# A hybrid decoder layer on one core: block products of an inverse taken tile by tile in turn, and norms of q by transposes

## The chip, the cores and the metric

The kernel runs on one core of a Trainium2 chip as one launch. The number that counts is the device time of that launch in microseconds (us). Five engines work side by side, each through its own instruction stream in order: TensorE (PE; its weight loads are shown apart as PEld), VectorE (DVE), ScalarE (ACT), GpSimd (POOL) and SyncE (SP), which only issues DMAs here. They wait for one another by semaphores.

## The reference

One decoder layer on 512 positions of width 1024, in float32. A wide input projection feeds two token mixers: a gated DeltaNet (8 heads of 128) and a gated linear recurrence (RG-LRU, 1280 channels). A gated merge, an output projection, a layer norm, a SwiGLU feed-forward part (width 2816) and a second layer norm follow. The part that matters here is the DeltaNet, cut to its core:

```
q = l2_normalize(q); k = l2_normalize(k)        # per position and head, over 128 channels
A = where(strict, (k*beta) @ k.T * decay, 0)    # per chunk and head
T_mat = A + I
sol = triangular_solve(T_mat, [v*beta, k*beta*exp(G)], lower=True, unit_diagonal=True)
o = (q*exp(G)) @ S + (q @ k.T * decay) @ v_new  # and S carried from chunk to chunk
```

## The kernel before

The large products stream 512 positions at a time: a weight block of 128x128 is loaded and a 128x512 operand runs through it. Each float32 product of that kind is taken as three matmuls (`mm3`, lines 154 to 157) on operands that ACT and POOL or DVE split into a high and a low part. A column job of 128 output columns is 8 such triples. The columns of the input projection come in the order of a table (`ORDER`), through `columns` and `play`.

The DeltaNet runs beside them, two heads at a time (four pairs, `dn_chain(p)`), with chunks of 128 positions instead of the reference's 64, so eight 128x128 matrices per pair (4 chunks, 2 heads). PE's program is written out by hand: `play` emits one triple, adds 0.68 to a planned clock and calls `advance`, which emits the next piece of each chain whose planned time has come. A chain gives, after each piece, the planned PE time of the piece and the latency until its result is to be there; the table `LAT` holds these latencies. So a larger number in `LAT` puts the next piece of that chain further down in PE's program, behind more triples; nothing waits by it. Each DVE and ACT instruction is placed by a scheduler, and one inside `with urgent()` gets a higher priority.

The inverse of T_mat is built from small blocks. A substitution on DVE inverts the 16x16 blocks on the diagonal (line 603 on, planned latency `sub`). Then PE doubles the block size: `m1` (line 632) and `m2` (line 644) go from 16 to 32 with products of 32x32 blocks, on four positions (0,0), (32,32), (64,64), (96,96) of the array; `i1`, `i2`, `i3` (lines 671, 683, 693) go from 32 to 64; `i4` and `i5` (lines 701, 710) go from 64 to 128 with 64x64 blocks. Each product stands 8 times, for the eight matrices, and float32 runs it as two passes. Before, a position is finished with all eight products, then triples of the projection follow, then comes the next position.

The norms of k (`norms`, line 490) transpose k on PE, square the transposed bank on ACT and sum it on DVE. The norms of q (`norms_q`, line 502) square q on ACT in the layout it has, and sum over the partitions with a product with ones on PE (tile `qn`, line 508). The result, after a reciprocal root on DVE, scales the output at the end of the chain.

PSUM banks outside the projections come from a ring of five (`bankd`): each use takes the next one, so a bank's new writer waits until the old content was read. `hold` takes a bank out of the ring and `give` puts it back at the end.

Of the kernel before, what the change touches and what calls it, by code (L numbers as in the profile page):

```python
# [8 lines left out]
F32 = mybir.dt.float32  # L9
F32R = mybir.dt.float32r  # L10
I32 = mybir.dt.int32
AF = mybir.ActivationFunctionType
ALU = mybir.AluOpType
# [7 lines left out]
         "z1 l3 v3 q3 g0 z2 g1 l4 g2 g3 z3 g4 g5 g6 g7")  # L21

LAT = {
    "F": 13.0, "kt": 12.0, "q": 5.2, "sq": 4.0, "qk": 1.0, "P": 4.0, "vt": 2.0, "u": 10.0, "sub": 29.0, "m1": 6.0,
    "m2": 8.0, "i2": 6.0, "i4": 7.0, "i5": 7.0, "x": 8.0, "ks": 5.0, "xr": 7.0, "su": 6.5, "ot": 26.0,
    "ba": 9.0, "g": 2.5, "conv": 11.0,
}

PIECE = 0.01
# [3 lines left out]
RMS_EPS = 1e-6  # L33
P = 128
# [7 lines left out]
CQ, CK, CV, CZ, CB, CA = 0, 1024, 2048, 3072, 4096, 4104  # L42
# [4 lines left out]
def layer_kernel(  # L47
# [9 lines left out]
    V, S, G, PE = nc.vector, nc.scalar, nc.gpsimd, nc.tensor  # L57

    const = ctx.enter_context(tc.tile_pool(name="const", bufs=1))
# [25 lines left out]
    def bank(ring, name):  # L85
        tag = rings[ring].pop(0)
        rings[ring].append(tag)
        return pp.tile([P, T], F32, tag=tag, name=name)
# [4 lines left out]
    def bankd(name):  # L93
        return bank("d", name)
# [46 lines left out]
    def rsqrt_seed(y, v):  # L141
        V.tensor_scalar(out=y.bitcast(I32), in0=v.bitcast(I32), scalar1=1, scalar2=None,
                        op0=ALU.logical_shift_right)
        V.tensor_scalar(out=y.bitcast(I32), in0=y.bitcast(I32), scalar1=-1.0,
                        scalar2=float(0x5F3759DF), op0=ALU.mult, op1=ALU.add)

    def rsqrt(y, v, w):
        rsqrt_seed(y, v)
        for _ in range(3):
            tt(V, w, y, y, ALU.mult)  # L150
            stt(w, w, -0.5, v, ALU.mult, ALU.mult)
            stt(y, w, 1.5, y, ALU.add, ALU.mult)
# [237 lines left out]
        V.tensor_scalar(out=c8n, in0=c8, scalar1=-1.0, scalar2=None, op0=ALU.mult)  # L390
        V.memset(tiny, 2.0 ** -110)

    ones = const.tile([P, 4], F32, name="ones")
    V.memset(ones, 1.0)
    eye32 = const.tile([P, 32], F32, name="eye32")
    for b in range(4):
        G.tensor_copy(out=eye32[32 * b:32 * b + 32],
# [45 lines left out]
    qkv = {}  # L443
# [33 lines left out]
    def dn_chain(p):  # L477
# [4 lines left out]
        sml = lambda n, name: small(n, f"{name}{p}", name)  # L482
# [7 lines left out]
        def norms(src, sq, n2, y, name):  # L490

            for j in range(2):
                ps = to_tok(src, j, f"{name}{p}_{j}")
                act(sq[:, j], ps, AF.Square)
                V.tensor_reduce(out=n2[:, 4 * j:4 * j + 4], in_=c4(sq[:, j]), axis=AX.X, op=ALU.add)
                yield j, ps
            V.tensor_scalar(out=n2, in0=n2, scalar1=RMS_EPS, scalar2=None, op0=ALU.add)
            rsqrt(y, n2, sml(8, f"{name}w"))

        c4 = lambda ps: ps.rearrange("p (c n) -> p c n", c=4)  # L500

        def norms_q(qT, sq, n2, y):

            act(sq, qT, AF.Square)
            yield 0.0, LAT["sq"]
            ps = bankd(f"qn{p}")
            for i in range(8):
                PE.matmul(ps[:, 4 * i:4 * i + 4], chunks(sq)[:, i], ones, start=True, stop=True)
            V.tensor_scalar(out=n2, in0=ps[:, 0:32:4], scalar1=RMS_EPS, scalar2=None, op0=ALU.add)
            rsqrt(y, n2, sml(8, "qtw"))  # L510


        yield from until("decay", *([f"k{p - 1}"] if p else []))
        yield from room(2)
        F, Fl = slot(f"F{p}"), slot(f"Fl{p}")
# [21 lines left out]
        nk, rk, nq, rq = (sml(8, n) for n in ("nk", "rk", "nq", "rq"))  # L537
# [12 lines left out]
        for j in range(2):  # L550
            ps = bankd(f"kk{p}_{j}")
            for c in range(4):
                i = 4 * j + c
                PE.matmul(ps[:, c * P:(c + 1) * P], kc[:, i], kc[:, i], start=True, stop=True)
            for c in range(4):
                i = 4 * j + c
                stt(Ac[:, i], ps[:, c * P:(c + 1) * P], br2[:, i:i + 1], Ac[:, i], ALU.mult, ALU.mult)

        def query_chain():
            yield from until(f"{CQ}_{p}")  # L560
            yield from room(1)
            sq, qc = slot(f"sq{p}"), chunks(qkv[CQ, p])
            yield from norms_q(qkv[CQ, p], sq, nq, rq)
            free(sq)
            yield 0.9, LAT["qk"]
            for j in range(2):
                ps = bankd(f"qk{p}_{j}")
                for c in range(4):
                    i = 4 * j + c
                    PE.matmul(ps[:, c * P:(c + 1) * P], kc[:, i], qc[:, i], start=True, stop=True)  # L570
                tt(V, Pm[:, j], ps, Pm[:, j], ALU.mult)
            done[f"q{p}"] = clock[0] + 1.8 + LAT["P"]
            yield 1.8, 0.0
# [26 lines left out]
        X, N = blk(xa, 0), blk(xa, 1)  # L600
        Xh, Ah, R, W = (half(xa, i) for i in (4, 5, 6, 7))
        for b in range(4):
            sl = slice(32 * b, 32 * b + 32)
# [19 lines left out]
        b8 = lambda ps, n: ps[:, :8 * n].rearrange("p (c n) -> p c n", c=8)  # L623
        yield from room(1)
        Yf = slot(f"Yf{p}")
        Yc = chunks(Yf)
        G.memset(Yf, 0.0)
        tag, ps = hold(f"m1{p}")
        for b in range(4):
            sl = slice(32 * b, 32 * b + 32)  # L630
            for i in range(8):
                PE.matmul(b8(ps, 32)[sl, i], N[sl, i], Y[sl, i], start=True, stop=True,
                          tile_position=(32 * b, 32 * b))
            if b < 3:
                yield 0.27, PIECE
        with urgent():
            V.tensor_copy(out=Z, in_=b8(ps, 32))
        give(tag)
        yield 0.27, LAT["m1"]
        tag, ps = hold(f"m2{p}")  # L640
        for b in range(4):
            sl = slice(32 * b, 32 * b + 32)
            for i in range(8):
                PE.matmul(b8(ps, 16)[sl, i], Z[sl, i], X[sl, i, 0:16], start=True, stop=True,
                          tile_position=(32 * b, 32 * b))
            if b < 3:
                yield 0.27, PIECE
        with urgent():
            tt(V, X[:, :, 0:16], X[:, :, 0:16], b8(ps, 16), ALU.subtract)
            V.transpose(out=rows_of(Y), in_=rows_of(X))  # L650
        give(tag)
        yield 0.27, LAT["m2"]
        done[f"s{p}"] = clock[0]
        yield from until(f"v{p}")
        vb = vbs[0]
# [2 lines left out]
        for b in range(4):  # L658
            sl = slice(32 * b, 32 * b + 32)
            G.tensor_copy(out=Yc[sl, :, sl], in_=Y[sl])  # L660
        X6c = flat(xa)[0:64, 256:768].rearrange("p (c n) -> p c n", c=8)
        G.memset(X6c[0:32, :, 32:64], 0.0)
        for b in range(2):
            sl = slice(32 * b, 32 * b + 32)
            G.tensor_copy(out=X6c[sl, :, sl], in_=X[sl])
        Qs = Y
        lohi = [(b, slice(b, b + 32), slice(b + 32, b + 64)) for b in (0, 64)]
        tag, ps = hold(f"i1{p}")
        for b, lo, hi in lohi:
            for i in range(8):  # L670
                PE.matmul(b8(ps, 32)[lo, i], Ac[hi, i, lo], Y[hi, i], start=True, stop=True,
                          tile_position=(b + 32, b))
            if b == 0:
                yield 0.27, PIECE
        with urgent():
            for b, lo, hi in lohi:
                V.tensor_copy(out=Qs[lo], in_=b8(ps, 32)[lo])
        give(tag)
        yield 0.27, LAT["i2"]
        tag, ps = hold(f"i2{p}")  # L680
        for b, lo, hi in lohi:
            for i in range(8):
                PE.matmul(b8(ps, 32)[lo, i], X[lo, i], Qs[lo, i], start=True, stop=True,
                          tile_position=(b, b))
            yield 0.27, PIECE
        with urgent():
            for b, lo, hi in lohi[::-1]:
                V.tensor_scalar(out=Yc[lo, :, hi], in0=b8(ps, 32)[lo], scalar1=-1.0, scalar2=None,
                                op0=ALU.mult)
        give(tag)  # L690
        ps = bankd(f"i3{p}")
        for i in range(8):
            PE.matmul(b8(ps, 32)[32:64, i], Qs[0:32, i], X[0:32, i], start=True, stop=True,
                      tile_position=(0, 32))
        with urgent():
            V.tensor_scalar(out=X6c[32:64, :, 0:32], in0=b8(ps, 32)[32:64], scalar1=-1.0, scalar2=None,
                            op0=ALU.mult)
        yield 0.27, LAT["i4"]
        ps = bankd(f"i4{p}")
        for i in range(8):  # L700
            PE.matmul(b8(ps, 64)[0:64, i], Ac[64:128, i, 0:64], Yc[64:128, i, 64:128], start=True, stop=True,
                      tile_position=(64, 0))
# [5 lines left out]
        ps = bankd(f"i5{p}")  # L708
        for i in range(8):
            PE.matmul(b8(ps, 64)[0:64, i], X6c[:, i], q6[i // 4][:, i % 4], start=True, stop=True,  # L710
                      tile_position=(0, 0))
        with urgent():
            V.tensor_scalar(out=Yc[0:64, :, 64:128], in0=b8(ps, 64)[0:64], scalar1=-1.0, scalar2=None,
                            op0=ALU.mult)
        vt, St = xa, A
# [5 lines left out]
        for c in range(4):  # L721
            ij = [c, 4 + c]
            if c > 0:
                ps = bankd(f"ks{p}_{c}").rearrange("p (j n) -> p j n", j=4)
# [6 lines left out]
            ps = bankd(f"xr{p}_{c}").rearrange("p (j n) -> p j n", j=4)  # L731
# [5 lines left out]
            if c < 3:  # L737
                ps = bankd(f"su{p}_{c}").rearrange("p (j n) -> p j n", j=4)
# [11 lines left out]
        qT = qkv[CQ, p]  # L750
        Pc, qc = chunks(Pm), chunks(qT)
# [29 lines left out]
        for j in range(2):  # L781
            ps = to_tok(obc, j, f"ot{p}_{j}")
# [289 lines left out]
    for i in range(4):  # L1072
        ps = bankp(f"mx1_{i}")
# [112 lines left out]
```

## Time and profile before

| | before |
|---|---|
| device time, median of 3 runs | 1060.07 us (1057.27 to 1061.66) |
| the profiled execution: device time | 1059.51 us |
| its span, first to last instruction | 1057.8 us |
| PE busy | 1032.3 us, 98% |
| DVE, ACT, POOL busy | 537.6, 426.3, 243.2 us |

A row of a view names the engine, the line of the kernel, the operation, the output and input tiles (buffer numbers left out), the shape and a count (x16). A matmul row counts passes: a float32 product of small blocks is two of them. Consecutive instructions of one kind are merged into one row; a row's duration reaches from the first start to the last end, and the ends of matmuls overlap with their successors, so the pace is read from start to start.

### The profile page before, as it was taken

To read this page: it belongs to the slowest core of one execution; us is meant where nothing else is said; L and a number is where in the kernel's file an instruction comes from. 1 tells how busy PE (TensorE), PEld (TensorE's weight loads), DVE (VectorE), ACT (ScalarE), POOL (GpSimd) and SP (SyncE) were. 2 spreads that over 40 slices of the span, in tenths; PEclk is the share of its full clock that TensorE was granted. 3 is DMA by queue.
4 is the path that set the end of the run, shared out by engine and by line. 5 is a ranking of instruction groups with operands and counts; after the bars stand their busy time and mean duration, and the time that the engine had idled before them with its cause. 6 is when DMAs were issued, how large, how long until landed. Compare 5 with 4: busy or idle time off the path is not lost. (4 is left out here: it accounts for less than half of the span.)

```text
span 1057.8 us, 14227 instructions
## 1 busy us (share of the span) xinstructions
PE 1032.3 (98%) x5662; PEld 848.0 (80%) x5662; DVE 537.6 (51%) x1154; ACT 426.3 (40%) x571; POOL 243.2 (23%) x234
## 2 busy tenths in 40 slices
PE   7999999999999999999999999899999999999996
PEld 4887777887887788878888888798888888888885
DVE  3769889645858482247133354933333333322426
ACT  4589256328523743485322224222222222221122
POOL 2373434423433333445400003000000000000006
PEclk9999899999999999999999999999999999999998
DMA  8332222212222222325333436203333433223322
GB/s 245 111 90 68 62 61 71 81 41 71 80 60 64 67 63 77 84 59 147 100 109 91 160 97 181 81 1 88 93 98 100 132 107 99 91 91 99 100 60 79
DMA packets 150662, 96.79 MB, mean 91 GB/s; under 512 B 4475, under 2 KB 139836, under 8 KB 150596
## 3 DMA queue, kind: packets, MB, share of 16 engines
q1 hardware_dynamic: 148064, 91.52, 30.0%
q0 software_dynamic: 1216, 4.20, 1.2%
q8 instruction: 44, 0.72, 0.3%
q10 hardware_dynamic: 1316, 0.16, 0.1%
q14 instruction: 22, 0.18, 0.1%
HBM read 93.76 MB, written 2.11 MB: 91 GB/s over the span
## 5 line engine op out<-in xcount | busy, mean ns | idle before, releaser
L135 ACT CAST wh<-wr 128x1024 fp32r<-128x1024 f32 x145 | 152.3, 1052 | 438.9 <-issue 150.4
L121 POOL TENSOR_TENSOR wl<-wr,wh 128x512 fp32r<-128x512 f32 x128 | 172.9, 1373 | 226.6 <-ACT wh L135 225.1
L121 DVE TENSOR_TENSOR wl<-wr,wh 128x1024 fp32r<-128x1024 f32 x81 | 99.2, 1225 | 209.5 <-ACT wh L135 209.5
L155 PE MATMUL pj<-xT,wh 128*128 128x512 f32 x224 | 93.6, 418 | 0.0
L157 PE MATMUL pj<-xT,wl 128*128 128x512 f32 x224 | 87.6, 391 | 0.0
L156 PE MATMUL pj<-xT,wh 128*128 128x512 f32 x224 | 87.5, 390 | 0.0
L127 ACT ACT_TABLE_LOAD x61 | 78.3, 1283 | 10.6 <-DMA rw<-in_lru_conv_w 7.5
L156 PE MATMUL dn<-wl,fT 128*128 128x512 f32 (+1 forms) x168 | 63.3, 377 | 0.0
L155 PE MATMUL dn<-wh,fT 128*128 128x512 f32 (+1 forms) x168 | 63.3, 377 | 0.0
L157 PE MATMUL dn<-wh,fT 128*128 128x512 f32 (+1 forms) x168 | 63.2, 376 | 0.0
L155 PE MATMUL fg<-hk,wh 128*128 128x512 f32 x160 | 62.3, 389 | 0.0
L156 PE MATMUL fg<-hk,wh 128*128 128x512 f32 x160 | 62.3, 389 | 0.0
L157 PE MATMUL fg<-hk,wl 128*128 128x512 f32 x160 | 62.2, 389 | 0.0
L155 PE MATMUL fu<-hk,wh 128*128 128x512 f32 x160 | 62.2, 389 | 0.0
L156 PE MATMUL fu<-hk,wh 128*128 128x512 f32 x160 | 62.2, 389 | 0.0
L157 PE MATMUL fu<-hk,wl 128*128 128x512 f32 x160 | 62.2, 389 | 0.0
L121 POOL TENSOR_TENSOR h<-h,g 128x512 f32<-128x512 f32 x6 | 8.1, 1357 | 193.2 <-ACT h L127 193.2
L155 PE MATMUL g<-xT,wh 128*128 128x512 f32 x128 | 51.4, 401 | 0.0
L157 PE MATMUL g<-xT,wl 128*128 128x512 f32 x128 | 50.0, 391 | 0.5 <-POOL wl L121 0.5
L156 PE MATMUL g<-xT,wh 128*128 128x512 f32 x128 | 49.9, 390 | 0.0
L157 PEld LDWEIGHTS pj<-xT,wl 128*128 128x128 f32 x224 | 42.1, 188 | 9.2
L155 PEld LDWEIGHTS pj<-xT,wh 128*128 128x128 f32 x224 | 42.1, 188 | 7.9 <-issue 0.2
(358 smaller groups left out, 2283.8 us busy)
## 6 DMA issues: line engine op xcount, KB each, us to landing
wr<-in_w_in SPq DMA_DIRECT2D x64, 512.0 KB, 3.9
wr<-in_w_ffn_gate SPq DMA_DIRECT2D x22, 512.0 KB, 3.8
wr<-in_w_ffn_up SPq DMA_DIRECT2D x22, 512.0 KB, 3.8
wr<-in_w_ffn_down SPq DMA_DIRECT2D x22, 512.0 KB, 3.7
wr<-in_w_branch_lru SPq DMA_DIRECT2D x8, 512.0 KB, 3.9
wr<-in_w_branch_dn SPq DMA_DIRECT2D x8, 512.0 KB, 4.6
wr<-in_w_out SPq DMA_DIRECT2D x8, 512.0 KB, 4.5
wk<-in_w_in SPq DMA_DIRECT2D x8, 256.0 KB, 6.3
```

What stands on the lines that cost most here:

```text
L121: return eng.tensor_tensor(out=o, in0=a, in1=b, op=op)
L127: return S.activation(out=o, in_=i, func=func, **kw)
L135: S.copy(out=hi, in_=src)
L155: PE.matmul(ps, wh, rh, start=start, stop=False)
L156: PE.matmul(ps, wh, rl, start=False, stop=False)
L157: PE.matmul(ps, wl, rh, start=False, stop=stop)
```

## The change

```diff
 LAT = {
-    "F": 13.0, "kt": 12.0, "q": 5.2, "sq": 4.0, "qk": 1.0, ... "sub": 29.0, "m1": 6.0,
+    "F": 13.0, "kt": 12.0, "q": 5.2, "qk": 5.0, ... "sub": 33.0, "m1": 7.0,
...
-    "ba": 9.0, "g": 2.5, "conv": 11.0,
+    "ba": 9.0, "g": 2.5, "conv": 14.0,
...
-    ones = const.tile([P, 4], F32, name="ones")
-    V.memset(ones, 1.0)
...
-        def norms_q(qT, sq, n2, y):
-
-            act(sq, qT, AF.Square)
-            yield 0.0, LAT["sq"]
-            ps = bankd(f"qn{p}")
-            for i in range(8):
-                PE.matmul(ps[:, 4 * i:4 * i + 4], chunks(sq)[:, i], ones, start=True, stop=True)
-            V.tensor_scalar(out=n2, in0=ps[:, 0:32:4], scalar1=RMS_EPS, scalar2=None, op0=ALU.add)
-            rsqrt(y, n2, sml(8, "qtw"))
...
-            yield from norms_q(qkv[CQ, p], sq, nq, rq)
+            for _ in norms(qc, sq, nq, rq, "qt"):
+                pass
...
+        quarters = [slice(32 * b, 32 * b + 32) for b in range(4)]
         tag, ps = hold(f"m1{p}")
-        for b in range(4):
-            sl = slice(32 * b, 32 * b + 32)
-            for i in range(8):
+        for i in range(8):
+            for b, sl in enumerate(quarters):
                 PE.matmul(b8(ps, 32)[sl, i], N[sl, i], Y[sl, i], start=True, stop=True,
                           tile_position=(32 * b, 32 * b))
-            if b < 3:
-                yield 0.27, PIECE
+            if i == 3:
+                yield 0.5, PIECE
...
-        yield 0.27, LAT["m1"]
+        yield 0.5, LAT["m1"]
...
-        tag, ps = hold(f"i1{p}")
-        for b, lo, hi in lohi:
-            for i in range(8):
+        ps = bankd(f"i1{p}")
+        for i in range(8):
+            for b, lo, hi in lohi:
                 PE.matmul(b8(ps, 32)[lo, i], Ac[hi, i, lo], Y[hi, i], start=True, stop=True,
                           tile_position=(b + 32, b))
-            if b == 0:
-                yield 0.27, PIECE
...
-        tag, ps = hold(f"i2{p}")
-        for b, lo, hi in lohi:
-            for i in range(8):
+        ps, p3 = bankd(f"i2{p}"), bankd(f"i3{p}")
+        for i in range(8):
+            for b, lo, hi in lohi:
                 PE.matmul(b8(ps, 32)[lo, i], X[lo, i], Qs[lo, i], start=True, stop=True,
                           tile_position=(b, b))
-            yield 0.27, PIECE
+            PE.matmul(b8(p3, 32)[32:64, i], Qs[0:32, i], X[0:32, i], start=True, stop=True,
+                      tile_position=(0, 32))
...
-        ps = bankd(f"i3{p}")
-        for i in range(8):
-            PE.matmul(b8(ps, 32)[32:64, i], Qs[0:32, i], X[0:32, i], start=True, stop=True,
-                      tile_position=(0, 32))
```

`m2` is changed as `m1` is. So the products of one matrix now stand on the two to four positions one after the other, then those of the next matrix; a piece of `m1` or `m2` holds 16 products (four matrices on four positions) instead of 8, `i1` is one piece of 16, and `i2` and `i3` are one piece of 24. Per pair, 13 pieces become 6. The norms of q go through `norms`, as those of k do.

The first place is PE's program in pair 0, from the norms of q to the norms of k of pair 1. `lw` are the gates of the recurrence, `lg` and `pj` columns of the projection, `qk` the products of k and q, `kt` the transposes of k of pair 1. Before:

```order
L825 MATMUL lw_1_0_812<-u_441,gr_444 128x512
...
L825 MATMUL lw_1_1_818<-u_441,gr_444 128x512
L508 MATMUL qn_856<-ones,sq_801 128x4 x8
...
L570 MATMUL qk_0_898<-x_0_430,x_0_404 128x128 x4
L570 MATMUL qk_1_904<-x_0_430,x_0_404 128x128 x4
...
L487 MATMUL kt_0_919<-ident,x_1_415 128x128 x4
L487 MATMUL kt_1_927<-ident,x_1_415 128x128 x4
```

And of the change:

```order
L807 MATMUL lw_0_0_796<-u_439,gr_442 128x512
L485 MATMUL qt_0_800<-ident,x_0_428 128x128 x4
L485 MATMUL qt_1_807<-ident,x_0_428 128x128 x4
...
L807 MATMUL lw_1_0_836<-u_439,gr_442 128x512
...
L807 MATMUL lw_1_1_842<-u_439,gr_442 128x512
...
L559 MATMUL qk_0_888<-x_0_428,x_0_402 128x128 x4
L559 MATMUL qk_1_894<-x_0_428,x_0_402 128x128 x4
...
L485 MATMUL kt_0_921<-ident,x_1_413 128x128 x4
L485 MATMUL kt_1_929<-ident,x_1_413 128x128 x4
```

Eight products with ones became eight transposes in two banks, and they stand earlier, behind the first of the four `lw`. Counted back five banks, the second bank of `kt` followed on `lw_1_1` before and follows on `lw_1_0` now.

The second place is PE's program in pair 0 from the end of `m1` (tile m_1082 or m_1115) to `m2` (m_1180 or m_1205). Before:

```order
L632 MATMUL m_1082<-xa_564 32x32 x8
L155 MATMUL pj_2_1_1137<-xT_132,wh_979 128x512
...
L487 MATMUL vt_0_1148<-ident,x_0_653 128x128 x4
L487 MATMUL vt_1_1154<-ident,x_0_653 128x128 x4
...
L157 MATMUL pj_2_1_1137<-xT_209,wl_980 128x512
L644 MATMUL m_1180<-xa_564 32x16 x8
L155 MATMUL lx_0_1196<-xT_132,wh_1022 128x512
```

And of the change:

```order
L622 MATMUL m_1115<-xa_562 32x32 x16
L155 MATMUL pj_2_1_1103<-xT_172,wh_981 128x512
...
L485 MATMUL vt_0_1170<-ident,x_0_651 128x128 x4
L485 MATMUL vt_1_1176<-ident,x_0_651 128x128 x4
...
L157 MATMUL lx_0_1189<-xT_172,wl_1025 128x512
L633 MATMUL m_1205<-xa_562 32x16 x16
L155 MATMUL lx_0_1189<-xT_183,wh_1024 128x512
```

`m2` began with the last triple of `pj_2_1` behind it and now begins five triples of `lx` later; `m1` ends later too. A row holds sixteen products where it held eight.

The third place is DVE's program where `m2` of pair 0 gets its bank: the products of k with k of pair 1 (`kk`, tile Fl) have to be read first. `x` are the convolution's taps on `pj_2_0`. Before:

```order
L637 COPY xa_564<-m_1082 128x256
...
L124 SCALAR_TENSOR_TENSOR Fl_757<-kk_0_1040,br_949,Fl_757 128x128
L124 SCALAR_TENSOR_TENSOR x_2_886<-pj_2_0_1027,cols,x_2_886 128x511
L124 SCALAR_TENSOR_TENSOR Fl_757<-kk_0_1040,br_949,Fl_757 128x128
L124 SCALAR_TENSOR_TENSOR x_2_886<-pj_2_0_1027,cols,x_2_886 128x510
...
L124 SCALAR_TENSOR_TENSOR Fl_757<-kk_1_1049,br_949,Fl_757 128x128 x4
```

And of the change:

```order
L124 SCALAR_TENSOR_TENSOR x_2_900<-pj_2_0_1029,cols,x_2_900 128x511
...
L124 SCALAR_TENSOR_TENSOR x_2_900<-pj_2_0_1029,cols,x_2_900 128x509
L627 COPY xa_562<-m_1115 128x256
...
L124 SCALAR_TENSOR_TENSOR Fl_755<-kk_0_1042,br_951,Fl_755 128x128 x4
L124 SCALAR_TENSOR_TENSOR Fl_755<-kk_1_1051,br_951,Fl_755 128x128 x4
```

The three taps moved ahead of the copy of `m1`. Ahead of the four `Fl<-kk_0` DVE has the same instructions as before and two TENSOR_REDUCE of 128x512 more (the sums of the norms of q); a small memset is gone.

## Rows read from the trace of the kernel before

**Rows 1.** The page: span, busy time of each engine, PE's granted clock in 40 slices.
```profile
span 1057.8 us, 14227 instructions
PE 1032.3 (98%) x5662; PEld 848.0 (80%) x5662; DVE 537.6 (51%) x1154; ACT 426.3 (40%) x571; POOL 243.2 (23%) x234
...
PEclk9999899999999999999999999999999999999998
```
**Rows 2.** PE's waits: line, releaser: us in total, times, longest.
```profile
PE kt L487 <- ACT ig L127: 2.0, 1, 2.0
...
PE ks L726 <- DVE Fl L124: 1.3, 2, 0.9
```
**Rows 3.** PE's groups by form: passes, busy us, mean ns of one.
```profile
L632 PE MATMUL m<-xa 32*32 32x32 f32 x256 | 11.0, 192 | 0.0
...
L671 PE MATMUL i<-xa,Fl 32*32 32x32 f32 x128 | 5.5, 192 | 0.0
...
L693 PE MATMUL i<-xa 32*32 32x32 f32 x64 | 2.7, 192 | 0.0
```
**Rows 4.** Timeline, m1 of pair 0 (start, us); last, line 632's loads (min/median/max ns).
```profile
105.29 0.69 PE L632 MATMUL m<-xa 32*32 32x32 f32 x16
105.91 0.50 PE L155 MATMUL pj<-xT,wh 128*128 128x512 f32 x1
106.24 0.39 PE L156 MATMUL pj<-xT,wh 128*128 128x512 f32 x1
106.47 0.40 PE L157 MATMUL pj<-xT,wl 128*128 128x512 f32 x1
106.80 0.69 PE L632 MATMUL m<-xa 32*32 32x32 f32 x16
...
105.29 0.58 PEld L632 LDWEIGHTS m<-xa 32*32 32x32 f32 x16 [0.37 <-issue]
...
L632 PEld LDWEIGHTS m<-xa x256: 101/108/108, 105.3 to 347.8; 32*32 32x32 f32 x128
```
**Rows 5.** Timeline of PE: norms of q, transposes of v, a group of i4.
```profile
81.66 1.84 PE L508 MATMUL qn<-ones,sq 128*128 128x4 f32 x16
83.36 0.48 PE L155 MATMUL lg<-xT,wh 128*128 128x512 f32 x1
...
112.63 1.03 PE L487 MATMUL vt<-ident,x 128*128 128x128 f32 x8
113.42 0.48 PE L155 MATMUL pj<-xT,wh 128*128 128x512 f32 x1
...
157.42 1.14 PE L701 MATMUL i<-Yf,Fl 64*64 64x64 f32 x16
```
**Rows 6.** Timeline of ACT and PE around the wait of kt.
```profile
85.30 0.69 ACT L127 ACTIVATE ig<-lw,cols 128x512 f32<-128x512 f32 x1
...
89.94 0.66 PE L487 MATMUL kt<-ident,x 128*128 128x128 f32 x4 [2.03 <-ACT ig L127]
```
**Rows 7.** Timeline of PE and DVE at m2 of pair 0; one reduce on DVE.
```profile
116.69 0.39 PE L157 MATMUL pj<-xT,wl 128*128 128x512 f32 x1
118.49 0.67 PE L644 MATMUL m<-xa 32*32 32x16 f32 x16 [1.41 <-DVE Fl L124]
...
118.09 1.37 DVE L124 SCALAR_TENSOR_TENSOR Fl<-kk,br,Fl 128x128 f32<-128x128 f32 x5
...
98.52 0.68 DVE L495 TENSOR_REDUCE nk<-xa 128x4 f32<-128x512 f32 x1
```
**Rows 8.** Stretches: us, busy of PE, PEld, DVE, ACT, POOL, PEclk, DMA.
```profile
77.50:119.40 41.90, 38.46 (x258) 30.68 (x257) 40.30 (x124) 27.55 (x33) 15.35 (x13) 1.00 0.26 69
...
117.00:120.00 3.00, 1.59 (x21) 1.08 (x20) 3.00 (x10) 1.73 (x3) 0.43 (x2) 1.00 0.34 101
120.00:130.20 10.20, 10.20 (x65) 7.72 (x65) 7.93 (x26) 1.46 (x3) 6.58 (x13) 0.50 0.19 53
...
165.00:187.00 22.00, 22.00 (x210) 16.67 (x209) 21.36 (x44) 12.70 (x15) 12.63 (x10) 1.00 0.27 73
```
**Rows 9.** Timeline of PE: two groups of m2 of pair 0.
```profile
119.98 1.03 PE L644 MATMUL m<-xa 32*32 32x16 f32 x16
...
122.52 1.03 PE L644 MATMUL m<-xa 32*32 32x16 f32 x16
```

More of the change, by code (lines that the diff above doesn't have):

```diff
@@ L23 @@
 LAT = {
-    "F": 13.0, "kt": 12.0, "q": 5.2, "sq": 4.0, "qk": 1.0, "P": 4.0, "vt": 2.0, "u": 10.0, "sub": 29.0, "m1": 6.0,
+    "F": 13.0, "kt": 12.0, "q": 5.2, "qk": 5.0, "P": 4.0, "vt": 2.0, "u": 10.0, "sub": 33.0, "m1": 7.0,
     "m2": 8.0, "i2": 6.0, "i4": 7.0, "i5": 7.0, "x": 8.0, "ks": 5.0, "xr": 7.0, "su": 6.5, "ot": 26.0,
-    "ba": 9.0, "g": 2.5, "conv": 11.0,
+    "ba": 9.0, "g": 2.5, "conv": 14.0,
 }
@@ L638, in dn_chain @@
         give(tag)
-        yield 0.27, LAT["m1"]
+        yield 0.5, LAT["m1"]
         tag, ps = hold(f"m2{p}")
-        for b in range(4):
-            sl = slice(32 * b, 32 * b + 32)
-            for i in range(8):
+        for i in range(8):
+            for b, sl in enumerate(quarters):
                 PE.matmul(b8(ps, 16)[sl, i], Z[sl, i], X[sl, i, 0:16], start=True, stop=True,
                           tile_position=(32 * b, 32 * b))
-            if b < 3:
-                yield 0.27, PIECE
+            if i == 3:
+                yield 0.5, PIECE
         with urgent():
@@ L651, in dn_chain @@
         give(tag)
-        yield 0.27, LAT["m2"]
+        yield 0.5, LAT["m2"]
         done[f"s{p}"] = clock[0]
@@ L677, in dn_chain @@
                 V.tensor_copy(out=Qs[lo], in_=b8(ps, 32)[lo])
-        give(tag)
-        yield 0.27, LAT["i2"]
-        tag, ps = hold(f"i2{p}")
-        for b, lo, hi in lohi:
-            for i in range(8):
+        yield 0.4, LAT["i2"]
+        ps, p3 = bankd(f"i2{p}"), bankd(f"i3{p}")
+        for i in range(8):
+            for b, lo, hi in lohi:
                 PE.matmul(b8(ps, 32)[lo, i], X[lo, i], Qs[lo, i], start=True, stop=True,
                           tile_position=(b, b))
-            yield 0.27, PIECE
+            PE.matmul(b8(p3, 32)[32:64, i], Qs[0:32, i], X[0:32, i], start=True, stop=True,
+                      tile_position=(0, 32))
         with urgent():
@@ L689, in dn_chain @@
                                 op0=ALU.mult)
-        give(tag)
-        ps = bankd(f"i3{p}")
-        for i in range(8):
-            PE.matmul(b8(ps, 32)[32:64, i], Qs[0:32, i], X[0:32, i], start=True, stop=True,
-                      tile_position=(0, 32))
         with urgent():
-            V.tensor_scalar(out=X6c[32:64, :, 0:32], in0=b8(ps, 32)[32:64], scalar1=-1.0, scalar2=None,
+            V.tensor_scalar(out=X6c[32:64, :, 0:32], in0=b8(p3, 32)[32:64], scalar1=-1.0, scalar2=None,
                             op0=ALU.mult)
-        yield 0.27, LAT["i4"]
+        yield 0.6, LAT["i4"]
         ps = bankd(f"i4{p}")
```

## The prediction

> **What bounds the kernel now.** I read the page first, then PE's waits, then PE's groups by form, then the timeline where small products stand, and last the stretches with their clock. On the page the reader is to see that PE is busy for 98% of the span and no other engine for more than 51% [rows 1]. PE's waits are few and short: 2.0 us at `kt`, 1.3 at `ks`, 1.4 at the first `m2` [rows 2, 7]. So what leaves PE's program leaves the time, unless a wait takes its place. PE's clock is at full speed except in the fifth slice and at the end [rows 1]; the stretches show where: at 120.0 it falls to 0.50, the lower of its two levels (1.2 of 2.4 GHz), for 10.2 us, after 3 us in which PE was busy for 1.59 [rows 8].
>
> The sum is made against the profiled execution: 1059.51 us with a span of 1057.8. The median of the three runs is 1060.07, so 0.56 is added at the end.
>
> **Fewer pieces of small products.** One piece of `m1` (8 products, 16 passes) and one triple repeat every 106.80 - 105.29 = 1.51 us. A matmul of the triple takes 106.47 - 106.24 = 0.23, the triple 0.68. So the piece costs 0.83. Its 16 loads take 0.58 in all; less 0.108 for the last one that is 0.47 for 15 steps, 0.0315 a pass, and 16 passes are 0.50. The other 0.33 is paid once per piece for going into small positions and back: 0.33 instead of 0.23 from the last `pj` to the first `m1`, the same behind the piece, and the rest at its edges [rows 4]. That is one price for all five kinds of piece, whose means are alike [rows 3]. The groups count 256 passes of `m1`, 128 of `i1`, 64 of `i3` [rows 3]; `m2` (16 columns, the same pace [rows 7]) has by the code as many as `m1`, and `i2` as many as `i1`: 832 passes, 52 pieces. The new code has 6 a pair, 24 in all. 28 x 0.33 = 9.2 us go.
>
> **Taking the positions by turns.** The passes stay 832. No row shows a change of position inside a piece, so this is bounded. Today a pass follows the columns of its weights and not those of its operand: 16 moving columns take as long as 32 [rows 4, 7], and 4 take (83.36 - 81.66)/16 = 0.106 us with 128 weight columns; 64 columns take (1.14 - 0.22)/15 = 0.061, with 0.22 for the last pass [rows 5]. Low end: the positions work side by side, four for the 512 passes of `m1` and `m2`, two for the 128 of `i1`, three for the 192 of `i2` and `i3`: 512 x 0.0315 x 3/4 + 128 x 0.0315 / 2 + 192 x 0.0315 x 2/3 = 18.1 us less. High end: each of the 416 changes of position (one per product) costs half of the 0.33 of a whole piece, 416 x 0.165 = 68.6 more. I take a value near the plain pace, because loads that stay serial gain next to nothing: by the paces above 32 columns are 0.0265 (from 128) to 0.0305 (from 64), so 0.001 to 0.005 of the 0.0315 is handing over; 0.0035 hidden at 416 changes is 1.5 us less.
>
> What a group shows here is a price at each entry into small positions. The Trainium skill, "TensorEngine Tiling (Array Packing)", section Key Properties, says that changing the tiling mode drains the array while changing only the tile does not, and that tiles load and multiply in parallel; by it the term would be near the low end, a result that stands among the rivals. The same page, section Restrictions and Gotchas, speaks against: row tiles are not to access one PSUM bank at the same time, and here four row tiles write one bank; by that the term would be nought. No run here shows either yet.
>
> **Norms of q.** The product with ones goes: 1.70 us for 16 passes [rows 5]. Eight transposes come, priced by those of v: 113.42 - 112.63 = 0.79 [rows 5]. 0.91 x 4 pairs = 3.6 us less on PE. ACT squares two banks of 512 instead of 1024 in one go, the same elements, off the path. DVE gets two reduces of 0.68 a pair [rows 7]; what they cost comes next.
>
> **Waits.** `kt` of pair 1 waited for its second bank until the last `ig` was read by ACT, 2.03 us; the order counted back five banks gives it now the bank of the first `ig`, read at 85.99 before [rows 6]. With two Squares in front, 0.7 each as that `ig`, it is 87.4. PE was there at 89.94 - 2.03 = 87.9 and comes 0.9 earlier by the norms, 87.0: 0.4 is left, 1.6 goes.
>
> `m2` of pair 0 waits for its bank until DVE has read the first half of `kk`. In the stretch up to there DVE is busy 40.30 of 41.90 us [rows 8], so it, not PE, sets that moment. Two reduces in front move it by up to 1.36, less the spare of 1.60, of which some lies behind waits that stay. PE comes later too: five triples more in front (3.4), two pieces fewer (0.6), norms (0.9), `kt` (1.6): 0.3 later. So the wait of about 1.5 (a matmul behind the start at 116.69 to 118.49, less the entry) [rows 7] becomes between 1.2 and 2.6; I take 2.1, 0.6 more. Behind the waiting `m2` on PE stand the triples of `lx`; nothing but the recurrence's later chain waits for those. The two together give 1.0 less.
>
> **The clock.** The drop stays: the same wait, no shorter, still stands ahead of the same `m2`. Its price: a piece of `m2` and a triple take 122.52 - 119.98 = 2.54 us in it [rows 9] and 1.51 outside [rows 4], so 10.2 x (1 - 1.51/2.54) = 4.1 us. It is in both sums.
>
> **Latencies.** `sub`, `m1`, `conv` and `qk` only move pieces down in PE's program. They cost nothing while triples remain to stand between: the last `ot` still stands ahead of columns of the merge gates and of `yl` in the new order, as before. SP's broadcast of the decays and POOL's masks move by a place or two, with more than 10 us until their use. If that cover were gone, the price is a wait like that at `ks`, 1.3 [rows 2].
>
> **The sum.** 9.2 + 1.5 + 3.6 + 1.0 = 15.3 us. 1059.5 - 15.3 = 1044.2, with 0.56 for the median 1045.
>
> **Rivals.** *Side by side.* The positions overlap fully: 18.1 instead of 1.5, 1028. For it: four positions use different partitions and their own weights. Against: a product's two passes share a position, and the loads at 0.0315 may come through one port. Anything between 1028 and 1040 counts here.
>
> *The clock falls in more places.* On the other side. A piece of `m1` or `m2` is now twice as long, two of them with a single triple between, at seven places beside the first `m2`. Where the clock falls at one, it costs 4.1. Four of them, 16.4, are more than the 15.3 gained: 1061, no longer faster, and from six on, 24.6, it is slower by over half a percent, 1069; all seven give 1073. For it: the fall came behind a stretch with little streaming, in such pieces. Against: from 165 to 187, with eight pieces of `m1` and `m2`, the clock was 1.00 throughout [rows 8]; only the wait distinguishes the fallen place.
>
> *A change of position costs like an entry.* The high end: 1044.2 + 1.5 + 68.6 + 0.6 = 1115. Against: within a piece the passes already follow at 0.0315 [rows 4] though each loads other weights.
>
> *DVE takes it back.* The reduces delay DVE's reads in every pair, not in pair 0 alone: DVE was busy for 21.36 of 22.00 us from 165 to 187 [rows 8]. Four times 1.36 and three more waits of 1.3 as at `ks` are 9.3: 1054. For it: the first `m2`. Against: DVE's total is 51% [rows 1].
>
> **How the numbers follow.** The forecast, 1040 to 1050 including a clock drop more or less, 55%. Side by side or part of it, 1028 to 1040, 25%. More falls of the clock, 1050 to 1073, 10%: 4 of them still faster, 4 no change, 2 slower. DVE, 1050 to 1060, 6%: 2 faster, 4 no change. Change of position, 4%, slower. Half a percent is 5.3 us, about what a measurement of this kernel can tell from no change. So faster 0.55 + 0.25 + 0.04 + 0.02 = 0.86, same 0.08, slower 0.06. The range leaves out the fullest overlap below (8%) and most of the clock's, DVE's and the last rival's ends above (10%): 1031 to 1056.
>
> **What would show it.** PE's passes of `qn` gone and 32 of `qt` there; 832 small passes in 24 pieces; pieces of 32 passes at about 1.3 us with their edges. A piece of 0.6 to 0.9 speaks for side by side, one of 3 or more for the costly change. The wait at `kt` under 1 us, that at the first `m2` between 1 and 3 with one clock drop behind it. I am wrong if PE's waits sum to over 5 us more than before, or if the clock falls in a second place.

## The result, and the profile after

The changed kernel takes 1030.26 us (median of 4 runs, 1029.83 to 1030.86), the kernel before on the same chip 1060.15 (4 runs, 1057.27 to 1061.66): a ratio of 0.9722, 95% interval 0.9700 to 0.9743. It is faster by 30 us. The forecast was 15 us, 1045, and the time lies 0.7 us below the range's low end: the sign was right, the size half of what it was. The profiled execution took 1029.83 us with a span of 1028.1, 29.7 less than before.

From the page: span, engines, the slices' granted clock (compare [rows 1]).

```profile
span 1028.1 us, 14179 instructions
PE 999.7 (97%) x5630; PEld 824.5 (80%) x5630; DVE 545.1 (53%) x1161; ACT 425.5 (41%) x576; POOL 247.6 (24%) x234
PEclk9999999999999999999999999999999999999998
```

PE is still the engine that sets the time, and the fifth slice, low before, is at full clock now. Next, PE's groups of small passes by form: count | busy us, mean ns of one | idle time before (compare [rows 3]).

```profile
L622 PE MATMUL m<-xa 32*32 32x32 f32 x256 | 3.6, 194 | 0.0
...
L660 PE MATMUL i<-xa,Fl 32*32 32x32 f32 x128 | 2.8, 192 | 2.0 <-DVE vb L121 2.0
```

One pass lasts as long as before, 192 to 194 ns from its start to its end, and there are as many of them. But 256 of `m1` cover 3.6 us of the engine where they covered 11.0: they lie on top of one another. The timeline of PE (start and length in us) in `m1` of pair 0 shows one whole period (compare [rows 4]), and beside it the transposes of q and the first `m2` (compare [rows 5, 7]), `i1` of pair 0, and `i2` with `i3` of pair 1:

```profile
76.26 1.03 PE L485 MATMUL qt<-ident,x 128*128 128x128 f32 x8
77.05 0.49 PE L155 MATMUL lg<-xT,wh 128*128 128x512 f32 x1
...
105.89 0.45 PE L622 MATMUL m<-xa 32*32 32x32 f32 x32
106.28 0.50 PE L155 MATMUL pj<-xT,wh 128*128 128x512 f32 x1
...
107.17 0.45 PE L622 MATMUL m<-xa 32*32 32x32 f32 x32
...
116.41 0.44 PE L633 MATMUL m<-xa 32*32 32x16 f32 x32 [1.53 <-DVE Fl L124]
...
127.32 0.69 PE L660 MATMUL i<-xa,Fl 32*32 32x32 f32 x32
127.95 0.51 PE L155 MATMUL lg<-xT,wh 128*128 128x512 f32 x1
...
197.46 0.22 PE L669 MATMUL i<-xa 32*32 32x32 f32 x2
197.48 0.21 PE L671 MATMUL i<-xa 32*32 32x32 f32 x1
197.52 0.20 PE L669 MATMUL i<-xa 32*32 32x32 f32 x2
197.53 0.19 PE L671 MATMUL i<-xa 32*32 32x32 f32 x1
...
198.09 1.16 PE L559 MATMUL qk<-x,x 128*128 128x128 f32 x8
```

A piece and a triple repeat every 107.17 - 105.89 = 1.28 us. Less the triple's 0.68, a piece of 32 passes costs 0.60; one of 16 cost 0.83. Take the 0.33 of going in and out off it, and 32 passes take 0.27, or 0.0084 each: about a quarter of the 0.0315 of before. `i1`, on two positions, has 32 passes from 127.32 to 127.95; add 0.20 for the edges outside that stretch (0.10 on each side of a piece, where a start comes 0.33 after the one before it instead of 0.23), and it is 0.83; less the same 0.33, that is 0.0156 a pass, a half. `i2` and `i3` take turns on three positions, and each product has two passes; their 48 passes last from 197.46 to 198.09, again 0.63, so 0.0104 a pass, a third. PE's waits, in us in total, times, longest:

```profile
PE i L669 <- DVE xa L664: 2.3, 2, 1.4
PE i L660 <- DVE vb L121: 2.0, 1, 2.0
PE m L633 <- DVE Fl L124: 1.5, 1, 1.5
...
PE ks L708 <- DVE Fl L725: 1.3, 1, 1.3
PE ks L708 <- DVE Fl L124: 1.3, 1, 1.3
PE kk L542 <- DVE rkb L121: 1.0, 1, 1.0
...
PE m L633 <- DVE xa L627: 0.6, 1, 0.6
```

These seven lines are 10.0 us in the recurrence, where `kt`, `ks` and `m2` had 4.7 [rows 2, 7]. The wait at `kt` is gone, five places have a new one. The stretches around the first `m2` and around the one place where the clock now falls (us; busy of PE, PEld, DVE, ACT, POOL; granted clock; DMA; compare [rows 8]):

```profile
116.00:120.00 4.00, 3.59 (x76) 2.79 (x77) 3.89 (x10) 0.34 (x1) 3.85 (x6) 1.00 0.10 15
...
245.00:249.00 4.00, 2.01 (x43) 1.73 (x43) 4.00 (x10) 3.98 (x10) 3.67 (x4) 0.99 0.00 0
249.00:252.40 3.40, 3.40 (x10) 2.66 (x9) 1.41 (x4) 3.36 (x5) 0.12 (x1) 0.52 0.58 154
```

Behind the first `m2` the clock stays at 1.00, though the wait there is 1.53 us. It falls to 0.52, the lower level, for 3.4 us at 249.0, after 4 us in which PE was busy for 2.01 and waited 2.0 at `i1` of pair 2.

A trace is one execution, and the clock is not the same in every execution of a kernel: the 16 of the kernel before on the chip of experiments 5 to 8 have mean granted clocks of 0.989 to 0.996 and times of 1062.3 to 1055.45 us, the faster ones at the higher clock. An estimate from the rows: the one at 0.996 took 1056.78 us, which leaves 8.5 us at half the clock, so the 10.2 us behind the first `m2` [rows 8] can't have been in it.

The account of the profiled 29.7 us, in the terms of the forecast:

| term | forecast | measured | from |
|---|---|---|---|
| fewer pieces, 28 x 0.33 | -9.2 | -9.2 | counted: 24 pieces instead of 52, at the forecast's price of 0.33 |
| positions by turns | -1.5 | -17.7 | `m1`, `m2`: 16 x 0.60 for 32 x 0.83; `i1`: 4 x 0.83 for 8 x 0.83; `i2` with `i3`: 4 x 0.83 for 12 x 0.83; together -26.9, less the 9.2 |
| norms of q on PE | -3.6 | -3.6 | 77.05 - 76.26 = 0.79 for eight transposes, 1.70 for the product |
| PE's waits in the recurrence | -1.0 | +5.3 | 10.0 and 4.7 |
| clock | 0 | -2.4 or somewhat more | the 4.1 of the old drop goes; a stretch of 3.4 us comes, whose loss is at most half of it, 1.7 |

These are -27.6 of 29.7; another 1.3 is a wait of PE ahead of the layer norm's transposes (`hp`, on DVE's `h`) that stood in the trace before and does not stand in the one after. Waits of PE at the start and at `g` are shorter by 1.2 in sum (`xp` 0.4, `psba` 0.3, `g` 0.5), which is more than the last 0.8. The first two terms are measured as one, 26.9; how it divides rests on the 0.33.

### The profile page after: what moved, and what is told of

Read it like the earlier page. It is cut to its first block, busy times and chain, and to the rows that moved or that the text cites. A ratio compares the mean times of both kernels' runs of the same rounds, so it can differ in the third digit from the quotient of the medians.

```text
span 1028.1 us, 14179 instructions
## 1 busy us (share of the span) xinstructions
PE 999.7 (97%) x5630; PEld 824.5 (80%) x5630; DVE 545.1 (53%) x1161; ACT 425.5 (41%) x576; POOL 247.6 (24%) x234
## 5 line engine op out<-in xcount | busy, mean ns | idle before, releaser
L127 ACT ACT_TABLE_LOAD x62 | 79.5, 1283 | 12.3 <-DMA rw<-in_lru_conv_w 6.8
L124 DVE SCALAR_TENSOR_TENSOR x<-pj,cols,x 128x511 f32<-128x511 f32 (+2 forms) x60 | 44.5, 742 | 9.9 <-ACT x L127 9.5
```

## Experiments

Each kernel ran with the kernel before beside it on its chip (medians of that 1058.97 to 1060.15), and ratios are to it. A difference to the changed kernel is one of medians across chips. "Pieces" is the time from the first start of each piece to the start of what follows it, summed over all of them: 32.9 us before, 12.3 after (of which 1.3 is waiting). "Waits" sums, between 30 and 545 us of the span, what lies between two starts on PE beyond the pace of the first one's kind, where that is over 0.45 us: 6.1 before, 11.2 after. It counts some gaps that the rows of waits leave out, so it is a little more than their sum; inside a low stretch it takes slow matmuls for waits, so experiments 4, 7, 8, 9, 11 and 12 are compared by the sum of the rows of waits in the recurrence, 10.0 after. "Low" lists the stretches at the lower clock outside start and end: 10.2 us at 120 before, 3.4 at 249 after.

**1. The turns alone.** The kernel before; the 52 pieces stay, but the eight blocks go round the positions. Shown for `m1`; `m2`, `i1` and `i2` alike.

```diff
-        for b in range(4):
-            sl = slice(32 * b, 32 * b + 32)
-            for i in range(8):
+        quarters = [slice(32 * b, 32 * b + 32) for b in range(4)]
+        for i in range(8):
+            for b, sl in enumerate(quarters):
                 PE.matmul(b8(ps, 32)[sl, i], N[sl, i], Y[sl, i], ...)
-            if b < 3:
+            if i in (1, 3, 5):
                 yield 0.27, PIECE
```

> The kernel before with one edit: within its 52 pieces of small products, whose number, length and place in PE's program stay, the products of one matrix go over the positions by turns. Theory 1 (positions work side by side: a pass costs 0.0315 us divided by the number of positions in turn): m1 and m2 save 512 x 0.0315 x 3/4 = 12.1 us, i1 and i2 (two positions) 256 x 0.0315 / 2 = 4.0, i3 nothing: 16.1 less, about 1044 us; a piece of m1 falls from 0.83 to about 0.45. If the half-clock stretch behind the first m2 goes as well, another 4 less, 1040. Theory 2 (loads are serial, what was gained is the number of pieces and the clock): a piece stays at about 0.8, 1.5 us less, 1058.

Measured 1044.31, ratio 0.9866 (0.984 to 0.9892). Pieces 16.6 instead of 32.9. Timeline of PE, one piece of `m1`:

```profile
107.91 0.33 PE L632 MATMUL m<-xa 32*32 32x32 f32 x16
108.17 0.50 PE L155 MATMUL pj<-xT,wh 128*128 128x512 f32 x1
```

0.26 from the piece's start to the triple's, where [rows 4] have 0.62. The 0.36 less is nearly the whole of 16 x 0.0315 x 3/4 = 0.38. Nothing else differs in that piece, so the order of the positions is worth this by itself, and side by side is shown. The trace, of the slowest of the four executions, also gives some back: waits 6.5, low 3.4 at 91, 6.8 at 122 and 3.4 at 272, in sum 3.4 us more than before.

The Trainium skill, "TensorEngine Tiling (Array Packing)", section Key Properties, has tiles loading and multiplying in parallel; the trace agrees, 0.0315 to 0.0084 a pass on four positions. The same page's section Restrictions and Gotchas says that row tiles cannot access one PSUM bank at the same time. Here four row tiles write one bank, each its own 32 partitions, at about a quarter of the time a pass, so for different partitions of a bank the measurement decides against it.

**2. The changed kernel without the turns.** Its 24 pieces, latencies and norms stay; within a piece it goes position after position.

```diff
-        for i in range(8):
-            for b, sl in enumerate(quarters):
+        for b, sl in enumerate(quarters):
+            for i in range(8):
                 PE.matmul(b8(ps, 32)[sl, i], N[sl, i], Y[sl, i], ...)
-            if i == 3:
+            if b == 1:
                 yield 0.5, PIECE
```

> The changed kernel with the products taken position by position inside its 24 longer pieces (the same pieces, latencies and norms). Theory 1: the passes go back to 0.0315 us each, 17 to 18 us more, about 1048 us, and a piece of m1 or m2 of 32 passes goes from 0.58 to about 1.33; if the half-clock stretch returns behind the first m2, 1052. Theory 2: within 2 us of the changed kernel, 1030 to 1032.

Measured 1039.82, ratio 0.9823 (0.9794 to 0.9853). Timeline of PE, `m1` of pair 0:

```profile
105.86 1.09 PE L622 MATMUL m<-xa 32*32 32x32 f32 x32
...
107.78 1.09 PE L622 MATMUL m<-xa 32*32 32x32 f32 x32
```

A period of 1.92, less 0.68, is 1.24 for a piece: the "about 1.3" of the forecast (0.33 + 32 x 0.0315 = 1.34), less 0.10 for its one change of position. So even a single change inside a piece gains, 0.10, where the bounds had up to 0.165 lost. Pieces are 26.1 in all, 13.8 more than after, but the kernel is only 9.6 slower than the changed one. PE's waits are 3.6 instead of 11.2: with slower pieces PE comes later to what it waits for. Against the turns stand 7.6 us of waits that they bring into the open, and against that again low stretches of 3.4 us at 119, 345 and 666 here.

**3. Norms by the product again.** The changed kernel; Square, product with ones and `LAT` "sq" 4.0, "qk" 1.0 as before.

```diff
-            for _ in norms(qc, sq, nq, rq, "qt"):
-                pass
+            yield from norms_q(qkv[CQ, p], sq, nq, rq)
```

> The changed kernel with the norms of q by the product with ones again (latencies sq 4 and qk 1). By the rows 3.6 us of PE come back; two reduces a pair leave DVE, so the waits of the first m2 (1.7) and of i1 and i2 (2.0 and 2.3) may shrink by up to 1.4 each. Theory 1 (PE bounds, DVE has room): about 1033.5 us. Theory 2 (DVE's reduces cost as much as PE gains): 1029 to 1031.

Measured 1042.81, ratio 0.985 (0.9829 to 0.9872). That is 12.5 us worse than the changed kernel, not the 3.6 of PE's work. PE's longest wait:

```profile
PE i L680 <- DVE xa L675: 6.0, 2, 5.2
```

Stretches ahead of and in the low stretch (columns as above):

```profile
136.00:141.70 5.70, 2.34 (x10) 1.61 (x9) 5.29 (x16) 4.05 (x4) 2.95 (x3) 1.00 0.68 192
141.70:148.60 6.90, 4.19 (x53) 2.76 (x54) 6.84 (x28) 0.69 (x1) 0.00 (x0) 0.51 0.13 40
```

`i2` of pair 0 waits 5.2 us for DVE's copy, until 143.62; the clock falls within that wait, at 141.7, for 6.8 us, and there are three more low stretches of 3.4. The wait at `kt` is back too, 2.0. Ahead of that copy DVE does the substitution of pair 1, and this begins later, at 124.95 where it was 120.01 after the change:

```profile
124.95 0.29 DVE L605 TENSOR_SCALAR xa<-xa,up 128x128 f32<-128x128 f32 x1 [2.60 <-POOL xa L604]
```

So with the product back DVE's chain comes later in pair 0, in part by a wait for POOL, and this costs more than the product; how the product leads to it was not followed.

**4 to 6. Latencies and norms one by one.** The changed kernel with the old planned latencies (4), the kernel before with the transposes and "qk" 5.0 (5), the kernel before with the new latencies (6).

```diff
 experiment 4, on the changed kernel
-    "sub": 33.0, "m1": 7.0, ... "conv": 14.0
+    "sub": 29.0, "m1": 6.0, ... "conv": 11.0
 experiment 5, on the kernel before
-            yield from norms_q(qkv[CQ, p], sq, nq, rq)
+            for _ in norms(qc, sq, nq, rq, "qt"):
+                pass
 experiment 6, on the kernel before
-    "sub": 29.0, "m1": 6.0, ... "conv": 11.0
+    "sub": 33.0, "m1": 7.0, ... "conv": 14.0
```

> The changed kernel with the planned latencies sub 29, m1 6 and conv 11 of the kernel before. Theory 1 (latencies only move pieces and PE has cover): within 1 us of the changed kernel, 1029 to 1031. Theory 2 (the longer latencies are what keeps PE from waiting, now that the pieces are short): PE's waits at m2, i2 and the transposes of v grow by 3 to 8 us, 1033 to 1038.

> The kernel before with the norms of q by transposes alone (latency qk 5). Theory 1 (the term of the prediction): 3.6 us of PE go, the wait of kt (2.2) falls under 1, that of the first m2 (1.6) grows by up to 1.4 because DVE has two reduces more in front: about 1055.5 us, with the half-clock stretch still there. Theory 2 (DVE sets the pace in pair 0, so what PE gains there turns into waits): 1057 to 1060.

> The kernel before with the planned latencies sub 33, m1 7 and conv 14 alone. Theory 1 (a longer latency is worth what it takes from PE's waits): the wait of the first m2 (1.6) goes, and with it the half-clock stretch of 10.2 us that follows (4.1): about 1054 to 1055 us. Theory 2 (the wait is not what drops the clock): 1058 to 1059, a half-clock stretch of about 10 us stays.

Measured: 4, 1039.09, ratio 0.9823 (0.9795 to 0.9851), so the old latencies cost the changed kernel 8.8 us: the waits sum to 15.2 instead of 10.0, and 13.6 us are low instead of 3.4. 5, 1059.93, ratio 1.0003 (0.9988 to 1.0019, 10 runs): no change. 6, 1054.2, ratio 0.9967 (0.9936 to 0.9999): a gain that the interval just tells from none (5.5 us by the medians, 3.5 by the ratio; one execution of the seven took 1064.48). PE's longest waits in 4, and the stretches around it:

```profile
PE m L633 <- DVE Fl L124: 6.3, 1, 6.3
PE ks L708 <- DVE Fl L124: 3.7, 1, 3.7
```

```profile
113.00:117.00 4.00, 0.86 (x4) 0.38 (x2) 3.73 (x10) 0.31 (x1) 2.30 (x2) 1.00 0.10 23
117.10:127.30 10.20, 7.17 (x78) 5.39 (x79) 8.23 (x25) 2.55 (x4) 4.66 (x9) 0.50 0.14 41
```

The same in 5, where the wait at `kt` went and the one at `m2` grew to 4.8:

```profile
115.00:119.00 4.00, 0.55 (x3) 0.12 (x1) 3.90 (x12) 0.36 (x1) 0.00 (x0) 0.98 0.47 131
119.00:132.60 13.60, 12.21 (x82) 9.07 (x83) 7.86 (x32) 2.82 (x5) 6.91 (x14) 0.50 0.14 40
```

And in 6 the stretch behind the first `m2`, which PE reaches without a wait:

```profile
120.00:130.20 10.20, 10.20 (x97) 7.70 (x96) 7.17 (x23) 2.65 (x4) 6.59 (x9) 1.00 0.19 51
```

In 5 the 3.6 us that PE saves return: `m2`'s wait is 3.4 longer, `vt` has a new one of 1.3, and the low stretch is 13.6 instead of 10.2 us. In 4 and in 5 it begins while PE still waits at `m2`: PE is busy for 0.86 and 0.55 of the 4 us ahead of it. In 6 the later order of `m1` and `m2` lets PE fill the wait with triples, and the low stretch behind `m2` is gone; 3.4 us at 205 and at 396 are what is left. So the longer latencies, priced at nothing, are part of whether the other parts keep what they gain.

**7. One piece instead of two.** The changed kernel; the triple between the halves of `m1` and of `m2` is taken out.

```diff
-            if i == 3:
-                yield 0.5, PIECE
...
-        yield 0.5, LAT["m1"]
+        yield 1.0, LAT["m1"]
```

> The changed kernel with m1 and m2 as one piece of 32 products each instead of two of 16: 16 pieces instead of 24. Theory 1 (0.33 us per entry into small positions): 8 x 0.33 = 2.6 less, about 1027.6 us. Theory 2 (a longer piece has no more than the cost of its passes, but DVE sets the pace around it): the waits at m2 and i2 (1.7 and 2.6) grow by as much, 1030.

Measured 1033.22, ratio 0.9752 (0.9728 to 0.9776), 3 us slower than the changed kernel, though the two intervals overlap. PE's waits at `m2`:

```profile
PE m L631 <- DVE Fl L124: 2.5, 1, 2.5
PE m L631 <- DVE xa L625: 2.2, 1, 2.2
```

Eight entries fewer are 8 x 0.33 = 2.6 us of work; `m2` now waits 2.5 and 2.2 where it waited 1.5 and 0.6. Other waits are shorter by as much (the sum is 10.1, 10.0 after), but there are three low stretches of 3.4 us instead of one, which cost up to 3.4 more. So the waits move, and the clock may take back more than the saved entries give; some 2 of the 3 us lost are not traced.

**8, 11, 12. Still longer latencies.** The changed kernel with all five below (8), with m1 alone (11), with i2 alone (12).

```diff
-    "kt": 12.0, ... "m1": 7.0, "m2": 8.0, "i2": 6.0, ... "ks": 5.0
+    "kt": 14.0, ... "m1": 9.0, "m2": 10.0, "i2": 9.0, ... "ks": 6.5
```

> The changed kernel with planned latencies longer still where PE waited after the change: kt 14, m1 9, m2 10, i2 9, ks 6.5. Theory 1 (these waits, 11.2 us in all, are PE coming too early for DVE's results and go when other triples stand in front): 6 to 9 us of waits less and the one half-clock stretch of 3.4 us gone, 1021 to 1024 us. Theory 2 (DVE is the bound there, so the waits move to the next dependent piece): 1028 to 1031.

> The changed kernel with m1 9 instead of 7 alone: three triples more between m1 and m2. Theory 1 (a wait is a matter of its own step): the first m2's wait of 1.7 and the second's of 0.8 go, the rest stays: 1027.5 to 1029. Theory 2 (each step later pushes the next ones onto other work of DVE and banks): 1030 to 1034.

> The changed kernel with i2 9 instead of 6 alone: four to five triples more between i1 and i2. Theory 1: the wait of i2 in pair 0 (2.6) goes, the rest stays: 1027.5 to 1028.5. Theory 2, as for m1: 1030 to 1034.

Measured 1035.82 (0.978; 0.9754 to 0.9806), 1035.55 (0.9783; 0.9759 to 0.9807) and 1033.29 (0.976; 0.9731 to 0.9789), 8 and 11 slower than the changed kernel, 12 by its median only, since its interval overlaps that one's. PE's longest waits of 8:

```profile
PE lw L807 <- DVE u L124: 4.6, 1, 4.6
PE su L722 <- DVE xa L717: 4.2, 1, 4.2
```

Of 11:

```profile
PE i L669 <- DVE xa L664: 4.7, 2, 4.5
```

In 11 the wait at the first `m2` is gone and the one at `i2` of pair 0, 1.4 after the change, is 4.5 long. In 12 that one is gone, and PE waits over 2 us at `ks` and `xr` in its place. The sum of the rows is 12.4 in 8, 10.2 in 11 and 10.5 in 12, against 10.0. A planned latency moves a wait of this chain; it doesn't take it away. What 11 loses is then hardly in the waits: 13.6 us are low there instead of 3.4, and half of the difference, the most that it can cost, is 5.1 of the 5.3 us lost (an estimate). In 8, 10.2 us are low. In 12 only 3.4 us are low; its trace is of the fastest execution, 1031.36.

**9. DVE without q's sums.** The changed kernel; the two reduces for the norms of q in each pair are small copies instead, so the scale of q isn't the layer's.

```diff
-                V.tensor_reduce(out=n2[:, 4 * j:4 * j + 4], in_=c4(sq[:, j]), axis=AX.X, op=ALU.add)
+                if name == "qt":
+                    V.tensor_copy(out=n2[:, 4 * j:4 * j + 4], in_=sq[:, j, 0:4])
+                else:
+                    V.tensor_reduce(...)
```

> The changed kernel without the sums over 128 channels in the norms of q: eight TENSOR_REDUCE of 0.68 us become copies of four columns, so the scale of q is not that of the layer. PE's program keeps its instructions. Theory 1 (DVE sets when PE may go on in pairs 0 and 1): the wait of the first m2 (1.7) goes to about 0.3, that of i2 of pair 0 (2.6) shrinks, 2 to 4 us less, 1026 to 1028. Theory 2 (these waits come from the order of instructions, not from DVE's load): within 1 us of the changed kernel, 1029 to 1031.

Measured 1030.62, ratio 0.9736 (0.9712 to 0.976): the time of the changed kernel. PE's waits at `i2` and `m2` have the same numbers as after, and so have those at `i1` and `ks`; the one at `kk`, 1.0, is gone:

```profile
PE i L672 <- DVE xa L667: 2.3, 2, 1.4
PE m L636 <- DVE Fl L124: 1.5, 1, 1.5
```

A row of DVE's timeline tells why: it now waits itself.

```profile
94.41 1.53 DVE L124 SCALAR_TENSOR_TENSOR x<-pj,cols,x 128x511 f32<-128x511 f32 x2 [1.09 <-ACT x L127]
```

After the change this row has 0.19 in place of 1.09. My theory that DVE's 1.36 us a pair for the norms set these waits falls for all but `kk`. DVE is held here by ACT's `x`, the read of a projection column, and ACT itself has no gap ahead of it from 87.63 on; how far that reaches was not followed.

The clock differs all the same. Behind the same waits at `i2` of pair 0 it falls here, where it stayed at 1.00 after the change, and it does not fall at 249, behind the same wait of `i1` of pair 2. The stretch at the lower clock here:

```profile
136.40:143.20 6.80, 6.39 (x55) 3.88 (x56) 6.71 (x33) 0.98 (x2) 0.00 (x0) 0.50 0.28 77
```

**10. The next blocks by turns too.** The changed kernel; the 64x64 products `i4` and `i5` go by turns over two positions. `i4`:

```diff
-        for i in range(8):
-            PE.matmul(b8(ps, 64)[0:64, i], ..., tile_position=(64, 0))
+        for c in range(4):
+            for h in range(2):
+                PE.matmul(b8(ps, 64)[64 * h:64 * h + 64, c], ..., tile_position=(64, 64 * h))
```

> The changed kernel with i4 and i5 on two positions of 64x64 by turns as well: matrices 4 to 7 of a pair take the other half of the partitions; one copy on DVE instead of one on DVE and one on ACT behind i4, two of half the size instead of one behind i5. Theory 1 (positions work side by side, for 64x64 too): a piece of i4 or i5 goes from 1.07 to about 0.6, 8 x 0.46 = 3.7 us less, 1026.5. Theory 2 (waits take it back, as with one piece for m1 and m2): 1029 to 1034.

Measured 1029.5 (1027.41 to 1032.08), ratio 0.9725 (0.9692 to 0.9759), the same as the changed kernel. Timeline of PE, `i5` of pair 0, first after the change, then in the experiment, and last `i4` of pair 0 in the experiment:

```profile
155.79 1.14 PE L692 MATMUL i<-xa 64*64 64x64 f32 x16
156.86 0.50 PE L155 MATMUL pj<-xT,wh 128*128 128x512 f32 x1
```

```profile
155.48 0.68 PE L697 MATMUL i<-xa 64*64 64x64 f32 x16
156.09 0.50 PE L155 MATMUL pj<-xT,wh 128*128 128x512 f32 x1
...
147.13 0.68 PE L687 MATMUL i<-Yf,Fl 64*64 64x64 f32 x16
147.74 0.50 PE L155 MATMUL lg<-xT,wh 128*128 128x512 f32 x1
```

1.07 becomes 0.61 in both, for eight groups 3.7 us of PE's work. Waits are 12.9 instead of 11.2, and a second low stretch of 3.4 us stands at 655; with up to 1.7 each that is 3.4 given back. The mechanism holds for the larger blocks, but here its gain does not reach the end of the program.

## Why the prediction was wrong

**The step that failed is "Taking the positions by turns".** It valued the turns at 1.5 us between bounds of -18.1 and +68.6, "because loads that stay serial gain next to nothing". The loads don't stay serial. Experiment 1 does only the turns and has 0.36 us less in a piece of 16 passes, and the account gives 17.7 us where the low bound had 18.1. That bound was worked out rightly; I took the value near today's pace because the rows show the loads one behind the other. But those rows show only passes on one position: they could not bear on what happens between positions, and the choice should have stayed open between the two ends. The rival "side by side", 25%, is what happened. That its 1028 comes so near the 1030 is in part luck: PE's waits are 6.3 us worse than its sum has them, and the clock and waits elsewhere, which it left alone, give over 4 back.

**Fewer pieces** was right: 24 pieces, and experiment 2, with the longer pieces and no turns, has 1.24 us for one of 32 passes, forecast 1.3.

**Norms of q** was right for PE's work, 3.6, but not for the time: alone it gains nothing (experiment 5), and to take it out of the changed kernel costs 12.5 (experiment 3).

**Waits** was wrong in sum and place. `kt` fell as forecast, and the first `m2` waits 1.5 (forecast 2.1). What I didn't see is that faster pieces themselves make waits: PE gets to `i2`, `i1`, `ks` and `kk` before DVE has what they need, 10.0 us instead of 4.7. "I am wrong if PE's waits sum to over 5 us more" is just met in the recurrence, 5.3; over all rows of PE's waits it is 2.8, 17.8 instead of 15.0. The reason is another than the rival's: DVE's reduces for q set only the 1.0 at `kk` (experiment 9).

**The clock** was wrong: "the drop stays" for the same wait. The wait stayed, the drop went. In experiments 4 and 5, where PE waits 6.3 and 4.8 us there, it falls again (and all ten executions of 5 have a mean clock of 0.990 or 0.991), so a long wait matters; after the change, with 1.5 us and pieces of 0.60, it doesn't; before, with 1.4 us and pieces of 0.83, it did. The wait alone does not decide: in experiment 2 it falls for 3.4 us behind a wait of 0.3 at this `m2`, experiment 9 has the waits of the changed kernel and other low places, and executions of one kernel differ. One trace was too little to count a drop on. That it falls in many more places, the rival, is not so after the change, one stretch instead of one; but the experiments have up to four.

**Latencies** were priced at nothing, and that was wrong: without them the changed kernel is 8.8 us slower (experiment 4), through longer waits at `m2`, `ks` and `vt` and the clock there.

The parts don't add up. From the kernel before, turns give 14.7, latencies 5.5 (3.5 by the ratio), norms nothing; taken out of the changed kernel they cost 9.6, 8.8 and 12.5. Each changes when PE comes to the four or five places at which it meets DVE, and the waits and the clock there follow.

What stays open: which read or write upstream sets DVE's lateness in pair 0 (ACT, which has no gap there in experiment 9, was not tried), and what exactly tells a wait after which the clock falls from one after which it doesn't.

## What to carry to other kernels

Products on blocks smaller than the array are worth ordering so that neighbours use different positions: a pass then costs the pace on one position divided by the number of positions in turn, whether or not entries are saved too. Where no row shows an operation, rows of passes that all share one position are no evidence for the serial end. When the engine that sets the time gets faster in a chain with another engine, add the waits at each meeting point anew, and try the planned latencies together with the edit, since they change how much of it is kept. Count the low stretches of the clock beside the waits, and look at several executions before putting a drop into a sum.

## What the runs showed of the hardware

- Four 32x32 positions on the diagonal follow each other at 0.0084 us a pass, two at 0.0156, three at about 0.010 (`i2` with `i3`), though one pass lasts 0.19 either way.
- The overlap doesn't ask for different row groups: `i3` at (0, 32) beside `i2` at (0, 0), and `i4` in experiment 10 at (64, 0) and (64, 64), get the division (48 passes on three positions in 0.63 us; 16 passes in 0.61 instead of 1.07).
- The lower clock came in stretches of 3.4 to 13.6 us; the longest began within PE's longest waits at `m2` (4.8 and 6.3 us: 13.6 and 10.2), but there a wait of 1.4 us was followed by 10.2 before, 1.5 by none after and 0.3 by 3.4 in experiment 2.
